# A written order for TensorE between the strided mix projection and the first feature tiles

## The chip, the cores and the metric

The kernel runs on one NeuronCore of a Trainium2 chip. The metric is the device time of one execution in microseconds (us), as the median over runs; lower is better. Below, TensorE (PE) multiplies matrices, VectorE (DVE) and ScalarE (ACT) work on elements and read TensorE's results from PSUM, GpSimd (POOL) works on elements in SBUF, and SyncE's queue (SP) issues the DMAs.

## The reference, cut to what matters

One encoder layer over 512 positions of width 1024, in float32: a mixer, then cross attention to 256 memory rows with 4 heads of width 256, then a gated feed-forward part, each followed by a LayerNorm over the sum with the scaled input. The stretch that is changed begins in the last part of the mixer's output projection and ends in the first features of the feed-forward part:

```
mixed = concat([rms_norm(out_a, g_win), rms_norm(out_b, g_dil)], -1)
h = layer_norm(ALPHA * h + mixed @ w_out, ln1_g, ln1_b)
mem_n = layer_norm(mem, mem_ln_g, mem_ln_b)
q = (h @ w_q).reshape(b, s, X_HEADS, X_HEAD_DIM)
k, v = the same of mem_n @ w_k and mem_n @ w_v
p = softmax(einsum('bshd,bmhd->bhsm', q, k) * X_HEAD_DIM ** -0.5)
o = einsum('bhsm,bmhd->bshd', p, v)
h = layer_norm(ALPHA * h + o.reshape(b, s, D_MODEL) @ w_o, ln2_g, ln2_b)
g = h @ w_gate            # then a convolution of width 3 along the positions
ff = (gelu(conv(g)) * (h @ w_up)) @ w_down
```

## The kernel before, in words

**Arithmetic.** A float32 product is computed as three products of a rounded part `hi` and a rest `lo`: hi x hi, hi x lo and lo x hi, all added in PSUM. So every operand exists as a pair. ScalarE makes `hi` by a copy (L139, L211, L1004), and VectorE or GpSimd makes `lo` by a subtraction (L141, L212, L1005). A weight tile of 128 x 1024 comes by one DMA of 512 KB into a `raw` buffer (three of them) and is split into `hi` and `lo` buffers (six of each). `w_cols` (L147) and `w_rows` (L152) do this; their argument `eng` names the engine for `lo`, VectorE if none is given.

**Tiles.** The 512 positions are four blocks of 128. A residual block `h[b]` holds 128 positions by 1024. `to_T` (L202) turns a block by eight transposes on TensorE (L206) into two PSUM banks; then come copies and subtractions (L211, L212) in two halves, into the pair `h1T` or `h2T` (`Uhi`, `Ulo`). `gemm_fm` (L162) multiplies 24 times with the positions as moving columns, `gemm_tm` (L173) 24 times with 512 weight columns moving. `layer_norm` (L131) takes statistics on VectorE, a reciprocal root on GpSimd (L112), and then two passes on VectorE in halves (L127, L129).

**PSUM.** There are eight banks: tag `g` two tiles of one bank, `t` and `o` one each, `s` two tiles of two banks. `f_tile` (L198) gives `t` and `g` by turns.

**The stretch.** The strided part of the mix projection (`mix_part`, L969 to L975) needs 12 matmuls for each half of each block; VectorE adds them to the residual, and norm and transposes of the block follow. The second half of the memory values (`proj_xv(1, ...)`, L978) stands behind this. The first three query tiles (L1055 to L1062) are computed in two halves of 256 positions, so that the first half needs only blocks 0 and 1; the others are whole. `attend_mem` (L1017) handles a head: for each block six matmuls of scores, a softmax (L1033 to L1039), two transposes (L1042), and for each pair of blocks the product with the values (L1049 to L1051) in 256 columns. The output projection (`proj_res_norm`, L983) runs over two column halves and four blocks; behind the second half come the norm and the transposes of each block. The first four feature products (two of `w_gate`, two of `w_up`) are computed in halves again (L1088 to L1096), and from feature 2 on (L1098) whole.

**What sets the order.** A planner places every instruction: it goes through the program with a timeline of its own and gives each engine, of what it holds to be ready, what stands first in the program. The engines then run their lists in that order. In a `manual_schedule` block the order of the named engine is that of the program text. Before the change such a block exists up to the end of the windowed part of the mix projection (L953); from the strided part on, the planner orders TensorE too, and moves matmuls of later stages ahead of waiting ones. DMAs are issued by SP in an order that the planner sets as well; a DMA whose buffer isn't free holds up those behind it.

Lines that the prediction names: L107 (the constants of a norm), L149 and L154 (weight loads), L160 (every matmul), L975 and L990 (PSUM onto the residual), L1109 to L1117 (a feature's evaluation), L1119 (constants of the last norm).

Of the kernel before, what the change touches and what calls it, by code (L numbers as in the profile page):

```python
# [13 lines left out]
ALU = mybir.AluOpType  # L14
# [59 lines left out]
def hymba_layer(ctx: ExitStack, tc: tile.TileContext, A, cst_d, out):  # L74
# [115 lines left out]
    gn = [0]  # L190

# [5 lines left out]

    def f_tile():  # L198
        gn[0] += 1
        return ps_tile("t", 1) if gn[0] % 3 == 1 else ps_tile("g", 2)  # L200
# [233 lines left out]
    def mmt(o, l, r, first, last, w=1.0):  # L434
        mm(o, l, r, first, last)
        tick(w)
# [324 lines left out]
    with tc.manual_schedule(engines={nc.tensor.engine}):  # L761
# [143 lines left out]
        def proj_xv(hf, pss):  # L905
            for i in range(KD // 2):
                w = w_rows(A["w_xv"][0], 2 * i, 2, hf * 512, 512)
                for b in range(2):
                    for k in (2 * i, 2 * i + 1):
                        whi, wlo = (t[:, k % 2, :] for t in w)  # L910
                        th, tl = (t[i][:, k % 2, b * P : (b + 1) * P] for t in memT)
                        mmt(pss[b], th, whi, k == 0, False)
                        mmt(pss[b], th, wlo, False, False)
                        mmt(pss[b], tl, whi, False, k == KD - 1)
            for b in range(2):
                nc.scalar.copy(vm[:, b, hf * 512 : (hf + 1) * 512], pss[b])
# [52 lines left out]
    wts = [load_dil(hf * 512) for hf in range(2)]  # L969
    for b in range(NB):  # L970
        for hf in range(2):
            ps = g_tile()
            mix_part(ps, wts[hf], b, 4, mm)
            hs = h[b][:, hf * 512 : (hf + 1) * 512]
            nc.vector.scalar_tensor_tensor(hs, ps, hp["d"][:, b : b + 1], hs, ALU.mult, ALU.add)  # L975
        layer_norm(h[b], g1, b1)
        to_T(h[b], h1T, b)
    proj_xv(1, [ps_tile("t", 1), ps_tile("o", 1)])  # L978

    def load_xo(c0, eng):  # L980
        return load_tm(A["w_xo"][0], c0, eng)

    def proj_res_norm(load, T, g, b_, dst):  # L983
        for hf in range(2):
            wts = load(hf * 512, nc.gpsimd)
            for b in range(NB):
                ps = f_tile()
                gemm_tm(ps, wts, T, blk(b))
                hs = h[b][:, hf * 512 : (hf + 1) * 512]
                nc.vector.scalar_tensor_tensor(hs, hs, ALPHA, ps, ALU.mult, ALU.add)  # L990
                if hf == 1:
                    layer_norm(h[b], g, b_)
                    to_T(h[b], dst, b)

    oT = T_pair()
    with pool("xat") as xp:
        w_xq = A["w_xq"][0]
        wq = {}

        def load_q(c):  # L1000
            wq[c] = w_cols(w_xq, c * P, nc.gpsimd)

        def split_ps(hi, lo, ps):
            nc.scalar.copy(hi, ps)  # L1004
            nc.vector.tensor_tensor(lo, ps, hi.bitcast(F32), ALU.subtract)  # L1005

        def evac_q(c, ps):
            wq["t", c] = [xpool.tile([P, S], F32R, tag="x", bufs=XB, name=n) for n in ("qh", "ql")]
            split_ps(*wq["t", c], ps)

        def proj_q(c):
            load_q(c)
            ps = f_tile()
            gemm_fm(ps, wq[c], h1T, 0, S)
            evac_q(c, ps)

        def attend_mem(hd):  # L1017
            qs = [wq["t", 2 * hd + cc] for cc in range(2)]
            kh, kl = split(kmT[:, 2 * hd : 2 * hd + 2, :], [P, 2, MEM], xpool, "x", XB, xpool, "x", XB)
            vh, vl = split(vm[:, :, hd * 256 : (hd + 1) * 256], [P, 2, 256], xpool, "x", XB, xpool, "x", XB)  # L1020
            for b2 in range(2):
                ph = xp.tile([P, 2, 256], F32R, tag="ph", bufs=2, name="ph")
                pl = xp.tile([P, 2, 256], F32R, tag="pl", bufs=2, name="pl")
                for b in (2 * b2, 2 * b2 + 1):
                    st_ = s_tile()
                    sp = st_[:, 0, :MEM]
                    t = slice(b * P, (b + 1) * P)
                    for cc in range(2):
                        mm(sp, qs[cc][0][:, t], kh[:, cc, :], cc == 0, False)
                        mm(sp, qs[cc][0][:, t], kl[:, cc, :], False, False)  # L1030
                        mm(sp, qs[cc][1][:, t], kh[:, cc, :], False, cc == 1)
                    mx = spool.tile([P, 1], F32, tag="mx", name="mx")
                    nc.vector.reduce_max(mx, sp, X, negate=True)  # L1033
                    nc.vector.tensor_scalar_mul(mx, mx, 1.0 / 16)
                    px = xp.tile([P, MEM], F32, tag="px", bufs=2, name="px")
                    dn = spool.tile([P, 1], F32, tag="dn", name="dn")
                    nc.scalar.activation(px, sp, AF.Exp, bias=mx, scale=1.0 / 16, accum_out=dn)
                    nc.vector.reciprocal(dn, dn)
                    nc.vector.tensor_scalar_mul(px, px, dn)  # L1039
                    tp = st_[:, 1, :MEM].rearrange("p (k t) -> p k t", k=2)  # L1040
                    for kb in range(2):
                        nc.tensor.transpose(tp[:, kb, :], px[:, kb * P : (kb + 1) * P], ident)  # L1042
                    t = slice((b % 2) * P, (b % 2 + 1) * P)
                    split_ps(ph[:, :, t], pl[:, :, t], tp)
                for cc in range(2):
                    ps = ps_tile("o", 1, [P, 256])
                    f = slice(cc * P, (cc + 1) * P)
                    for kb in range(2):
                        mm(ps, vh[:, kb, f], ph[:, kb, :], kb == 0, False)  # L1049
                        mm(ps, vh[:, kb, f], pl[:, kb, :], False, False)  # L1050
                        mm(ps, vl[:, kb, f], ph[:, kb, :], False, kb == 1)  # L1051
                    t = slice(b2 * 256, (b2 + 1) * 256)
                    split_ps(oT[0][:, 2 * hd + cc, t], oT[1][:, 2 * hd + cc, t], ps)

        first = [f_tile() for _ in range(3)]  # L1055
        for c in range(3):
            load_q(c)
        for s2 in range(2):
            for c in range(3):
                gemm_fm(first[c][:, s2 * 256 : (s2 + 1) * 256], wq[c], h1T, s2 * 256, 256)  # L1060
        for c in range(3):
            evac_q(c, first[c])  # L1062
        proj_q(3)
        attend_mem(0)
        proj_q(4)
        proj_q(5)
        attend_mem(1)
        proj_q(6)
        proj_q(7)
        attend_mem(2)  # L1070
        attend_mem(3)

    g2, b2 = gb_tiles(A["ln2_g"][0], A["ln2_b"][0])
    h2T = U_pair()
    proj_res_norm(load_xo, oT, g2, b2, h2T)
    mid.close()

    fp = ctx.enter_context(pool("ffn"))
# [118 lines left out]
```

## Time and profile before

| what | value |
|---|---|
| median of 3 runs | 975.44 us (975.24 to 977.02) |
| the profiled execution | 976.09 us, of which its span 974.0 |
| TensorE busy | 926.4 us, 95% |
| VectorE, ScalarE, GpSimd busy | 490.2, 366.4, 206.4 us |
| mean granted TensorE clock | 0.978 |
| HBM | 88.34 MB read, 4.19 MB written, 95 GB/s |

The page gives busy time for each engine, the chain of work that ended last, and groups of instructions by line. Rows of the order of time read: start, duration, engine, line, operation, output<-inputs, count, and in brackets the idle time before it with what ended it. The ends of matmuls are modelled: a row's duration runs past the start of the next one, so the distance of two starts is the cost of a matmul. `hi`, `lo` and `raw` are weight tiles, `Uhi` and `Ulo` the turned residual, `Thi` and `Tlo` the turned mix or attention output, `qh` and `ql` query tiles.

### The profile page before, as it was taken

What the parts mean: (1) busy time and instruction counts of PE and PEld (TensorE: products, weight loads), DVE (VectorE), ACT (ScalarE), POOL (GpSimd) and SP (SyncE); (2) the same over time, 40 slices, a digit from 0 to 9 for tenths busy, and PEclk for the clock granted to TensorE, in tenths of its full rate; (3) what the DMA queues carried; (4) which work ended last, traced back from release to release, by engine and by line L of the source; (5) the groups of instructions that cost most, each with busy time, mean ns of one, the idle gap of its engine ahead of it and who ended that gap; (6) DMA issues with size and microseconds to landing.
All of it is one profiled execution on the core that took longest, in us unless ns stands there. A gap on an engine that the chain in (4) does not pass through costs nothing.

```text
span 974.0 us, 12289 instructions
## 1 busy us (share of the span) xinstructions
PE 926.4 (95%) x4825; PEld 770.1 (79%) x4825; DVE 490.2 (50%) x866; ACT 366.4 (38%) x645; POOL 206.4 (21%) x135
## 2 busy tenths in 40 slices
PE   7989999999998899899899997999999999999996
PEld 5777887788776698688887786988888888788885
DVE  6683334524444564749435648454434443333346
ACT  3453444335544557322334512433323332232310
POOL 4253114511443232424541043000000000000001
PEclk7999999999999899999999997999999999999999
DMA  9542032313221227432531034233333333223201
GB/s 320 163 152 65 22 108 66 87 44 108 66 66 47 62 88 214 132 102 58 155 119 44 1 87 130 70 107 104 92 101 95 97 98 98 98 87 108 87 22 65
DMA packets 117066, 93.33 MB, mean 96 GB/s; under 512 B 12471, under 2 KB 100751, under 8 KB 117008
## 3 DMA queue, kind: packets, MB, share of 16 engines
q1 hardware_dynamic: 115106, 90.33, 30.6%
q10 hardware_dynamic: 1902, 2.21, 0.7%
q8 instruction: 38, 0.62, 0.3%
q14 instruction: 20, 0.16, 0.1%
HBM read 88.34 MB, written 4.19 MB: 95 GB/s over the span
## 4 chain that ended last, share of the span: by engine, by line
PE 59%; DVE 5%; ACT 2%; issue 2%; POOL 1%; DMA 0%; DVEq 0%; ACTq 0%; POOLq 0%
PE g L160 25%; PE s L160 15%; PE acc L160 12%; PE t L160 3%; PE o L160 2%; DVE h L129 1%; POOL lo L141 0%; ACT hi L139 0%; DVE lo L141 0%; PE s L206 0%; ACT pu L596 0%; PE t L505 0%; DMA raw<-in_w_xq_dram 0%; PE o L513 0%; DVE ka L704 0%
## 5 line engine op out<-in xcount | busy, mean ns | idle before, releaser
L139 ACT CAST hi<-raw 128x1024 fp32r<-128x1024 f32 x148 | 155.3, 1050 | 249.2 <-PE g L160 161.9
L141 DVE TENSOR_TENSOR lo<-raw,hi 128x1024 fp32r<-128x1024 f32 x114 | 141.7, 1244 | 147.8 <-ACT hi L139 145.7
L141 POOL TENSOR_TENSOR lo<-raw,hi 128x1024 fp32r<-128x1024 f32 x34 | 84.8, 2506 | 121.5 <-ACT hi L139 120.9
L112 POOL TENSOR_TENSOR rs<-ve,mhalf 128x1 f32<-128x1 f32 x18 | 15.6, 868 | 416.6 <-DVE ve L118 416.6
L160 PE MATMUL g<-Thi,hi 128*128 128x512 f32 x240 | 97.6, 407 | 2.1 <-DVE zs L367 2.1
L160 PE MATMUL g<-Thi,lo 128*128 128x512 f32 x240 | 97.0, 404 | 0.0
L160 PE MATMUL g<-Tlo,hi 128*128 128x512 f32 x240 | 96.7, 403 | 0.0
L160 PE MATMUL g<-Ulo,hi 128*128 128x512 f32 (+1 forms) x248 | 91.9, 371 | 1.1 <-DVE Ulo L212 1.0
L160 PE MATMUL g<-Uhi,hi 128*128 128x512 f32 (+1 forms) x248 | 91.7, 372 | 0.6 <-ACT Uhi L211 0.5
L160 PE MATMUL g<-Uhi,lo 128*128 128x512 f32 (+1 forms) x248 | 91.5, 369 | 0.0
L368 POOL TENSOR_TENSOR zs<-zs,rsn 128x512 f32<-128x512 f32 x29 | 57.5, 1983 | 148.4 <-DVE zs L367 148.4
L160 PE MATMUL g<-hi,Thi 128*128 128x512 f32 x200 | 82.7, 414 | 0.5 <-ACT Thi L299 0.3
L160 PE MATMUL g<-hi,Tlo 128*128 128x512 f32 x200 | 81.3, 408 | 1.8 <-DVE Tlo L327 1.8
L160 PE MATMUL g<-lo,Thi 128*128 128x512 f32 x200 | 78.5, 398 | 0.0
L160 PE MATMUL s<-Uhi,hi 128*128 128x512 f32 (+1 forms) x192 | 71.3, 371 | 0.0
L160 PE MATMUL s<-Ulo,hi 128*128 128x512 f32 (+1 forms) x192 | 71.3, 371 | 0.0
L160 PE MATMUL s<-Uhi,lo 128*128 128x512 f32 (+1 forms) x192 | 71.3, 371 | 0.0
L160 PE MATMUL acc<-hi 128*128 128x512 f32 x176 | 68.6, 390 | 0.8 <-DVE act L1117 0.8
L160 PE MATMUL acc<-hi,lo 128*128 128x512 f32 x176 | 68.5, 389 | 0.0
L160 PE MATMUL acc<-lo,hi 128*128 128x512 f32 x176 | 68.5, 389 | 0.0
L160 PEld LDWEIGHTS g<-Thi,hi 128*128 128x128 f32 x240 | 45.8, 191 | 13.5 <-DVE zs L367 2.9
L160 PEld LDWEIGHTS g<-Ulo,hi 128*128 128x128 f32 x248 | 48.8, 197 | 8.7 <-DVE Ulo L212 1.6
(259 smaller groups left out, 1737.4 us busy)
## 6 DMA issues: line engine op xcount, KB each, us to landing
raw<-in_w_in_dram SPq DMA_DIRECT2D x38, 512.0 KB, 3.9
raw<-in_w_gate_dram SPq DMA_DIRECT2D x22, 512.0 KB, 3.8
raw<-in_w_up_dram SPq DMA_DIRECT2D x22, 512.0 KB, 3.9
raw<-in_w_down_dram SPq DMA_DIRECT2D x22, 512.0 KB, 3.3
raw<-in_w_xk_dram SPq DMA_DIRECT2D x8, 512.0 KB, 3.9
raw<-in_w_xv_dram SPq DMA_DIRECT2D x8, 512.0 KB, 3.3
raw<-in_w_xq_dram SPq DMA_DIRECT2D x8, 512.0 KB, 4.1
raw<-in_w_xo_dram SPq DMA_DIRECT2D x8, 512.0 KB, 3.3
```

Source lines behind the costliest of these rows:

```text
L112: nc.gpsimd.tensor_tensor(out_, in_, mhalf, ALU.pow)
L129: nc.vector.scalar_tensor_tensor(th[i], th[i], rs, bt[i], ALU.mult, ALU.add)
L139: nc.scalar.copy(hi, raw)
L141: (eng or nc.vector).tensor_tensor(lo, raw, hi.bitcast(F32), ALU.subtract)
L160: nc.tensor.matmul(o, l, r, start=first, stop=last)
L368: nc.gpsimd.tensor_tensor(sh, sh, rsn, ALU.mult)
```

## The change

From the strided mix projection to the halves of the first features the program stands in `manual_schedule` blocks for TensorE, and its text is put into a new order:

- Mix: blocks 0, 1, 2, then the transposes of block 0, mix of block 3, transposes of block 1; first halves of three query tiles; transposes of block 2; three quarters of the second half of the memory values (now in one `s` tile); transposes of block 3; the last quarter; second halves of the query tiles.
- Cross attention by head, in four steps: `kv` splits keys and values, `x_scores` computes the scores of four blocks into one `s` tile and takes the softmax by pairs of blocks (one reduction for two), `x_turn` transposes all of a head's eight tiles into one `s` tile, `x_pv` multiplies with the values over all 512 positions into `o` and `t`. Query projections and other heads' steps stand between these.
- The softmax tiles `px` use the two buffers `gb`, which also hold the constants of the norms; the second norm's constants are loaded after them.
- Output projection: in the first column half, blocks 0 to 2 first take the six tiles of heads 0 to 2 and, behind head 3, the other two. In the second half the transposes of a block stand one to three stages behind its matmuls; those of blocks 2 and 3 stand between the feature products.
- The four feature products use `t`, `o`, `g`, `g` instead of `g`, `s`, `g`, `s`; the transpose of the convolution's weights stands behind the second of them.
- The weight tiles of the queries, the output projection and the first features are split by VectorE instead of GpSimd; those of the strided mix stay on GpSimd. `f_tile` is gone.

The core of the diff (the old stretch is printed above):

```
+        def proj_xv(hf, pss, i0=0, i1=KD // 2):
+            for i in range(i0, i1):
+                xv_rows(i, hf, pss, w_rows(A["w_xv"][0], 2 * i, 2, hf * 512, 512))
...
+    def proj_q(c):
+        ps = g_tile()
+        gemm_fm(ps, w_cols(w_xq, c * P), h1T, 0, S)
+        evac_q(c, ps)
...
+    def x_scores(hd):
+        kh, kl = KV[hd][0:2]
+        s = s_tile().rearrange("p a (c k) -> p (a c) k", c=2)
+        px = wpool.tile([P, NB, MEM], F32, tag="gb", bufs=2, name="px")
+        st_x[hd] = px
+        for b2 in range(2):
+            for b in (2 * b2, 2 * b2 + 1):
+                t = slice(b * P, (b + 1) * P)
+                for cc in range(2):
+                    qh, ql = QT[2 * hd + cc]
+                    mm(s[:, b, :], qh[:, t], kh[:, cc, :], cc == 0, False)
+                    mm(s[:, b, :], qh[:, t], kl[:, cc, :], False, False)
+                    mm(s[:, b, :], ql[:, t], kh[:, cc, :], False, cc == 1)
+            mx, dn = (spool.tile([P, 2], F32, tag=n, name=n) for n in ("mx", "dn"))
+            nc.vector.reduce_max(mx, s[:, 2 * b2 : 2 * b2 + 2, :], X, negate=True)
+            nc.vector.tensor_scalar_mul(mx, mx, 1.0 / 16)
...
+    def x_turn(hd):
+        px = st_x[hd]
+        tp = s_tile()
+        hl = st_x["t", hd] = [xp.tile([P, 2, S], F32R, tag=n, bufs=1, name=n) for n in ("ph", "pl")]
+        for kb in range(2):
+            for b in range(NB):
+                nc.tensor.transpose(tp[:, kb, b * P : (b + 1) * P], px[:, b, kb * P : (kb + 1) * P], ident)
+        for kb in range(2):
+            split_ps(hl[0][:, kb, :], hl[1][:, kb, :], tp[:, kb, :])
+
+    def x_pv(hd):
+        ph, pl = st_x["t", hd]
+        vh, vl = KV[hd][2:4]
+        pss = [ps_tile("o", 1), ps_tile("t", 1)]
+        for kb in range(2):
+            for cc in range(2):
+                f = slice(cc * P, (cc + 1) * P)
+                mm(pss[cc], vh[:, kb, f], ph[:, kb, :], kb == 0, False)
+                mm(pss[cc], vl[:, kb, f], ph[:, kb, :], False, False)
+                mm(pss[cc], vh[:, kb, f], pl[:, kb, :], False, kb == 1)
...
+    with tc.manual_schedule(engines={nc.tensor.engine}):
+        wts = [load_dil(hf * 512) for hf in range(2)]
...
+        dil(0)
+        dil(1)
+        dil(2)
+        to_T(h[0], h1T, 0)
+        dil(3)
+        to_T(h[1], h1T, 1)
+        first = [ps_tile("t", 1), g_tile(), g_tile()]
+        wq = [w_cols(w_xq, c * P) for c in range(3)]
+        for c in range(3):
+            gemm_fm(first[c][:, 0:256], wq[c], h1T, 0, 256)
+        to_T(h[2], h1T, 2)
+        xv = s_tile()
+        xv = [xv[:, i, :] for i in range(2)]
+        proj_xv(1, xv, 0, 3)
+        to_T(h[3], h1T, 3)
+        proj_xv(1, xv, 3, 4)
+        for c in range(3):
+            gemm_fm(first[c][:, 256:512], wq[c], h1T, 256, 256)
+            evac_q(c, first[c])
+        oT = T_pair()
+        kv(0)
+        x_scores(0)
+        proj_q(3)
+        x_turn(0)
+        kv(1)
+        x_scores(1)
+        x_pv(0)
+        proj_q(4)
+        x_turn(1)
+        proj_q(5)
+        x_pv(1)
+        kv(2)
+        x_scores(2)
+        proj_q(6)
+        x_turn(2)
+        proj_q(7)
+        x_pv(2)
+        kv(3)
+        x_scores(3)
+        w_xo = A["w_xo"][0]
+        wo = load_tm(w_xo, 0)
...
+        part = [g_tile(), g_tile()]
+        gemm_tm(part[0], wo, oT, blk(0), 0, 6)
+        x_turn(3)
+        gemm_tm(part[1], wo, oT, blk(1), 0, 6)
+        x_pv(3)
+        part.append(s_tile()[:, 0, :])
+        gemm_tm(part[2], wo, oT, blk(2), 0, 6)
+        for b in range(3):
+            gemm_tm(part[b], wo, oT, blk(b), 6, 8)
+            xo_evac(b, 0, part[b])
+        ps = ps_tile("t", 1)
+        gemm_tm(ps, wo, oT, blk(3))
+        xo_evac(3, 0, ps)
...
+        g2, b2 = gb_tiles(A["ln2_g"][0], A["ln2_b"][0])
+        h2T = U_pair()
+        wo = load_tm(w_xo, 512)
...
+        xo_1(0)
+        xo_1(1)
+        xo_1(2)
+        to_T(h[0], h2T, 0)
+        xo_1(3)
+        to_T(h[1], h2T, 1)
+        mid.close()
...
+    with tc.manual_schedule(engines={nc.tensor.engine}):
+        pre = [[None, ps_tile("t", 1)], [None, ps_tile("o", 1)], [None, g_tile()], [None, g_tile()]]
...
+        pre_gemm(0, 0)
+        pre_gemm(1, 0)
+        tp = s_tile()[:, 0, 0:88]
+        nc.tensor.transpose(tp, cw, ident[0:88, 0:88])
+        nc.vector.tensor_copy(cwT, tp)
+        to_T(h[2], h2T, 2)
+        pre_gemm(2, 0)
+        to_T(h[3], h2T, 3)
+        pre_gemm(3, 0)
+        for i in range(4):
+            pre_gemm(i, 1)
```

More of the change, by code (lines that the diff above doesn't have):

```diff
@@ L188, in ps_tile @@
         return gpool.tile(shape or [P, 512], F32, tag=tag, bufs=bufs, name=tag)
-    gn = [0]
     def g_tile():
@@ L196, in s_tile @@
         return ps_tile("s", 2, [P, 2, 512])
-    def f_tile():
-        gn[0] += 1
-        return ps_tile("t", 1) if gn[0] % 3 == 1 else ps_tile("g", 2)
     def to_T(t, T, b):
@@ L968, in hymba_layer @@
     h1T = U_pair()
-    wts = [load_dil(hf * 512) for hf in range(2)]
-    for b in range(NB):
-        for hf in range(2):
-            ps = g_tile()
[L973 to L1076, printed above, removed]
+    xs = ExitStack()
+    xp = xs.enter_context(pool("xat"))
+    w_xq = A["w_xq"][0]
+    QT = {}
+    KV = {}
+    st_x = {}
+    def split_ps(hi, lo, ps):
+        nc.scalar.copy(hi, ps)
+        nc.vector.tensor_tensor(lo, ps, hi.bitcast(F32), ALU.subtract)
+    def x2(shape, names):
+        return [xpool.tile(shape, F32R, tag="x", bufs=XB, name=n) for n in names]
@@ new lines, in evac_q, with kv @@
+    def evac_q(c, ps):
+        QT[c] = x2([P, S], ("qh", "ql"))
+        split_ps(*QT[c], ps)
+    def proj_q(c):
+        ps = g_tile()
+        gemm_fm(ps, w_cols(w_xq, c * P), h1T, 0, S)
+        evac_q(c, ps)
+    def kv(hd):
+        k_ = split(kmT[:, 2 * hd : 2 * hd + 2, :], [P, 2, MEM], xpool, "x", XB, xpool, "x", XB)
+        v_ = split(vm[:, :, hd * 256 : (hd + 1) * 256], [P, 2, 256], xpool, "x", XB, xpool, "x", XB)
+        KV[hd] = k_ + v_
+    def x_scores(hd):
[14 more added lines that the diff above has]
+            nc.vector.tensor_scalar_mul(mx, mx, 1.0 / 16)
+            for i in range(2):
+                b = 2 * b2 + i
+                nc.scalar.activation(
+                    px[:, b, :], s[:, b, :], AF.Exp, bias=mx[:, i : i + 1], scale=1.0 / 16,
+                    accum_out=dn[:, i : i + 1],
+                )
+            nc.vector.reciprocal(dn, dn)
+            for i in range(2):
+                b = 2 * b2 + i
+                nc.vector.tensor_scalar_mul(px[:, b, :], px[:, b, :], dn[:, i : i + 1])
@@ new lines, in x_turn @@
+    def x_turn(hd):
[17 more added lines that the diff above has]
+                mm(pss[cc], vh[:, kb, f], pl[:, kb, :], False, kb == 1)
+        for cc in range(2):
+            split_ps(oT[0][:, 2 * hd + cc, :], oT[1][:, 2 * hd + cc, :], pss[cc])
```

54 lines of the change are left out of this document (30 added, 24 removed).

## The prediction

> **What bounds the kernel now.** I read the page first, then the table of stretches, then TensorE's order of time around each stretch that loses something.
>
> ```profile
> span 974.0 us, 12289 instructions
> PE 926.4 (95%) x4825; PEld 770.1 (79%) x4825; DVE 490.2 (50%) x866; ACT 366.4 (38%) x645; POOL 206.4 (21%) x135
> ```
>
> TensorE (PE) is busy for 95% of the span, and the chain of waits runs mostly through it. So only time in which TensorE stands still or runs slowly can be won, and only where the change reaches. The change reaches from the first matmul of the strided mix projection (about 428 us) to the last of the first feature tiles (about 627.7 us). Columns of the next view: stretch, its length, then busy time of PE, PEld, DVE, ACT, POOL (with counts), granted PE clock, DMA share, GB/s.
>
> ```profile
> 468.60:476.40 7.80, 5.10 (x30) 4.75 (x29) 5.08 (x4) 1.17 (x2) 3.14 (x2) 0.78 0.67 182
> 476.40:509.50 33.10, 33.10 (x192) 29.23 (x192) 8.21 (x16) 12.44 (x19) 14.31 (x6) 1.00 0.35 117
> 509.50:560.40 50.90, 47.87 (x289) 40.14 (x287) 31.09 (x95) 24.43 (x68) 4.79 (x2) 1.00 0.08 25
> ...
> 591.50:606.10 14.60, 8.89 (x40) 8.20 (x40) 14.60 (x24) 2.22 (x3) 5.46 (x4) 0.65 0.62 184
> ...
> 428.00:627.70 199.70, 188.09 (x1081) 164.07 (x1080) 119.41 (x222) 71.23 (x131) 57.59 (x28) 0.97 0.28 83
> ```
>
> Busy time hides short pauses, so I price the work itself, from rows where TensorE runs without a break: the chain's piece of 24 matmuls of 512 columns, the first and last of 33 matmuls of 256 columns, and a group of eight transposes with what follows it.
>
> ```profile
> 633.34 5.44 PE s L160 x24
> ```
> ```profile
> 623.75 0.28 PE L160 MATMUL g<-Uhi,hi 128*128 128x256 f32 x1
> ...
> 627.59 0.28 PE L160 MATMUL s<-Uhi,lo 128*128 128x256 f32 x1
> ```
> ```profile
> 583.49 1.03 PE L206 MATMUL s<-cst,h 128*128 128x128 f32 x8
> 584.28 0.47 PE L160 MATMUL g<-hi,Thi 128*128 128x512 f32 x1
> ```
>
> That is 5.44/24 = 0.227 us for 512 columns, 3.84/32 = 0.120 us for 256, and 0.79/8 = 0.099 us for a transpose. The loops of the code between the two ends issue 456 matmuls of 512 columns (96 strided mix, 48 memory values, 120 queries, 192 output), 528 of 256 (144 queries, 96 scores, 96 times values, 192 features) and 97 transposes: 103.4 + 63.4 + 9.6 = 176.4 us. The stretch took 199.7. So 23.3 us are lost, and that is the most that any order can win here. Where they are lost:
>
> ```profile
> 469.63 0.63 PE L206 MATMUL s<-cst,h 128*128 128x128 f32 x4 [0.86 <-issue]
> 472.35 0.66 PE L206 MATMUL s<-cst,h 128*128 128x128 f32 x4 [1.85 <-DVE h L129]
> 473.12 0.42 PE L160 MATMUL g<-Uhi,lo 128*128 128x256 f32 x1
> 473.34 0.42 PE L160 MATMUL g<-Uhi,hi 128*128 128x256 f32 x1
> ```
> ```profile
> 595.77 1.85 PE L206 MATMUL s<-cst,h 128*128 128x128 f32 x8 [4.18 <-DVE h L129]
> 598.29 0.80 PE L160 MATMUL g<-Uhi,hi 128*128 128x256 f32 x2 [0.53 <-ACT Uhi L211]
> 600.09 0.58 PE L160 MATMUL g<-Ulo,hi 128*128 128x256 f32 x1 [1.00 <-DVE Ulo L212]
> ```
>
> Both LayerNorm ends have one shape: the transposes wait for VectorE's last step of the norm (L129), and then the clock is low (0.78 and 0.65), so that 256 columns take 0.22 us instead of 0.12. In 468.6 to 476.4, 22 matmuls of 256 and 8 transposes are worth 3.4 us: 4.4 lost. In 591.5 to 606.1, 31 matmuls and 9 transposes are worth 4.6: 10.0 lost. The other 8.9 are shared by cross attention (3.0 shown as idle in 509.5 to 560.4) and short pauses that busy time hides; 476.4 to 509.5, q projections alone, has no idle time.
>
> **The change part by part.** *TensorE's work.* Only the product with the values changes: 96 matmuls of 256 columns (11.5 us) become 48 of 512 (10.9). That is -0.6.
>
> *Weight splits leave GpSimd.* The `lo` halves of 20 weight tiles (8 of w_xq, 8 of w_xo, 4 of the first features) move to VectorE. What one costs on each engine, and what GpSimd's did to the norm:
>
> ```profile
> L141 DVE TENSOR_TENSOR lo<-raw,hi 128x1024 fp32r<-128x1024 f32 x9 | 11.0, 1220 | 14.6 <-ACT hi L139 14.6
> ```
> ```profile
> L141 POOL TENSOR_TENSOR lo<-raw,hi 128x1024 fp32r<-128x1024 f32 x20 | 50.0, 2513 | 87.8 <-ACT hi L139 87.2 <-POOL rs L112 0.5
> ```
> ```profile
> 466.59 5.16 POOL L141 TENSOR_TENSOR lo<-raw,hi 128x1024 fp32r<-128x1024 f32 x2
> ```
> ```profile
> 444.50 0.75 DVE L975 SCALAR_TENSOR_TENSOR h<-g,rad__3380,h 128x512 f32<-128x512 f32 x1 [0.64 <-PE g L160]
> 445.29 0.69 DVE L134 BATCH_NORM_STATS2 st<-h 128x6 f32<-128x512 f32 x1
> ...
> 446.33 1.41 DVE L127 SCALAR_TENSOR_TENSOR h<-h,mv,gb 128x512 f32<-128x512 f32 x2
> ...
> 448.91 0.74 DVE L129 SCALAR_TENSOR_TENSOR h<-h,rs,gb 128x512 f32<-128x512 f32 x1
> ...
> 467.17 5.12 DVE L129 SCALAR_TENSOR_TENSOR h<-h,rs,gb 128x512 f32<-128x512 f32 x2
> ```
>
> VectorE gets 20 x 1.22 = 24.4 us more. In return the pair of L129, which under GpSimd's two splits took 5.12 us, has no split beside it; undisturbed, such a pair is worth 1.41 like L127. A norm from the PSUM result to the finished block is then 444.50 to 449.65 less the 0.6 of another block's step in between: 4.5 us.
>
> *First norm.* New order: three blocks of mix, transposes of block 0, the fourth block, transposes of block 1, half of three q projections (72 x 0.12 = 8.6 us), transposes of block 2, three quarters of the memory values (36 x 0.227 = 8.2), transposes of block 3. Block 3 now has 0.8 + 8.6 + 0.8 + 8.2 = 18.4 us, and a wait for block 1, against a norm of 4.5: the old wait and its low clock go (-4.4). What is late next: the q projection right behind the transposes of block 1 needs their halves. From the two engines' rows of such a hand-over:
>
> ```profile
> 584.56 0.59 ACT L211 CAST Uhi<-s 128x512 fp32r<-128x512 f32 x1 [9.07 <-PE s L206]
> 585.90 0.59 ACT L211 CAST Uhi<-s 128x512 fp32r<-128x512 f32 x1 [0.76 <-DVE Ulo L212]
> ```
> ```profile
> 585.18 0.69 DVE L212 TENSOR_TENSOR Ulo<-s,Uhi 128x512 fp32r<-128x512 f32 x1 [4.08 <-ACT Uhi L211]
> ```
>
> TensorE is free at 584.28 and the first half is there at 585.87: 1.6 us. The second half comes 1.35 later, under 12 matmuls (1.44). Nothing covers the 1.6; behind that matmul on TensorE stands everything else. VectorE also has more per mix block (2 x (0.75 + 0.69) + 0.4 + 2 x 1.41 = 6.1 us) than TensorE (5.44), the values no longer lie between the blocks, and there are only two `g` banks. The lag is 0.7 a block, plus 1.4 for block 0's halves and 2.4 for two q weights: about 5 at the fourth block, against 2.7 us (the other bank) + 0.8 of cover. So 0 to 2.5; I take 1.0, nearer none, because the planner may put the bank's step ahead. New loss 1.6 + 1.0 = 2.6. Net -1.8.
>
> *Cross attention.* Softmax of a pair of blocks, first step to last, in today's trace (VectorE):
>
> ```profile
> 499.14 0.43 DVE L1033 TENSOR_REDUCE mx<-s 128x1 f32<-128x256 f32 x1 [3.15 <-PE s L160]
> ...
> 501.19 0.35 DVE L1039 TENSOR_SCALAR px<-px,dn 128x256 f32<-128x256 f32 x1
> ...
> 492.89 0.69 DVE L1005 TENSOR_TENSOR ql<-t,qh 128x512 fp32r<-128x512 f32 x1 [4.67 <-ACT qh L1004]
> ```
>
> That is 2.4 us; with one reduction for both blocks ahead of the first exponential, at most 0.43 more: 2.8. Its transposes now come a projection (5.44) later, or at the last head 18 matmuls (4.08): covered. The values product comes after 2.9 us at head 0, and later elsewhere, against two hand-overs of 1.35. Tightest is head 1's scores, which need q tile 3 just 0.8 us after its projection; today the `ql` of that tile is ready at 493.58, 2.1 us after its last matmul: 0 to 1.3, I take 0.5, and as much again for the other heads. Some 17 changes of stage at 0.08 (0.31 instead of 0.227 us for the first matmul behind transposes) are 1.4. Of the 8.9 lost outside the norms I keep 1.9 as now, plus 1.4 and 1.0 to 1.2: 4.5. Saved 4.4; bounds 1.8 (the shown 3.0 idle goes, and q tile 3 costs its 1.3) and 6.5 (only 2.4 stays).
>
> *Loads.* The norm's constants share their two buffers with the softmax tiles now, so their DMAs wait on SP's queue for the transposes of heads 2 and 3, and four w_xo loads stand behind them. Cover: 90 matmuls of 512 from those transposes to the second half of w_xo, 20.4 us.
>
> ```profile
> raw<-in_w_xo_dram SPq DMA_DIRECT2D x8, 512.0 KB, 3.3
> ```
>
> Five such transfers in a row are 16.5, with a split 18.9: nothing, by 1.5 us. Past that cover it costs what it is late.
>
> *Second norm.* Behind the third output block stand transposes 0, block 3's matmuls, transposes 1, two feature halves (5.8), transposes 2, one half (2.9), transposes 3: 18.2 us with the 1.6 wait for block 1. VectorE's work in that time is two norms (2 x 4.5), three blocks' halves (3 x 1.4), at most four splits (4.9): 18.1. It fits, barely. So -10.0, and new: 1.6, plus one step of the norm (0.7) in VectorE's queue ahead of it, 2.4 with its hand-over; bounds 1.6 and 3.8. Net -7.6.
>
> *Feature banks.* Feature 2 needs the bank of feature 1's gate, behind which only 24 x 0.12 = 2.9 us of matmuls lie. Today those three steps take 621.59 to 624.38, 2.8 us:
>
> ```profile
> 621.59 0.77 ACT L1109 ACTIVATE c<-g,cwT 128x512 f32<-128x512 f32 x1
> ...
> 623.63 0.75 DVE L1113 SCALAR_TENSOR_TENSOR c<-g,cwT,c 128x511 f32<-128x511 f32 x1
> ```
>
> I take +0.2; bounds 0 and 1.2 (a split in front).
>
> **The sum.** -0.6 - 1.8 - 4.4 - 7.6 + 0.2 = -14.2. The profiled execution took 976.1 for a span of 974.0, so 2.1 lie around it; 974.0 - 14.2 + 2.1 = 961.9. It was 0.65 above the median of 975.44: 961.2.
>
> **Rivals.**
> (a) *The new waits lower the clock.* The trace shows it low after pauses of 0.86 and 1.85 within 4 us, and shows the attention stretch, with 3.0 us of pauses scattered over 51, at 1.00. The new waits of 1.6 to 2.6, in one piece, lie between. A low clock met 22 matmuls at the first norm and 31 at the second, at 0.1 us each 2.2 and 3.1: 961.2 + 5.3 = 966. [...]
> (b) *The waits move instead of going.* If VectorE, whose 18.1 of 18.2 us has no reserve, comes 5 us late to block 3's second norm, that and one low clock give back 7.6, and the time is 969. For it: the margin. Against: TensorE also slips by its own waits, which gives VectorE time.
> (c) *Slower.* The 24.4 us of splits stand in VectorE's in-order queue ahead of hand-overs that TensorE's fixed order can no longer step around. All on the path: 961.2 + 24.4 = 986. It decides from 14.2/1.22 = 12 of the 20 splits. For it: every hand-over passes VectorE. Against: VectorE is busy 119.4 of 199.7 us, and splits are asked for early.
>
> **Chances.** The forecast 0.62 (own range, from the bounds: 957 to 968), (a) 0.15, (b) 0.15, (c) 0.08. A measurement here tells about 0.2% from no change, 973.5 to 977.4. Faster 0.88, same 0.04 (the edges of b and c), slower 0.08. The range goes from 955.5 to 971, so that it holds (a) and (b) and leaves out (c) and the outer edges.
>
> **What would show it.** Right: no wait on L129 ahead of transposes; two waits of 1.6 to 2.6 us for Uhi or Ulo, behind block 1's transposes of each norm; granted clock near 1.00 throughout; the stretch from the first strided mix matmul to the last half-width feature matmul about 185.5 us; GpSimd with nothing but the root and four splits. Wrong: a pause over 3 us anywhere in it, a low clock (a), a transposes wait on L129 for block 3 (b), or waits on L141 splits adding to over 10 us (c).

## The result, and the profile after

| | before | changed |
|---|---|---|
| median | 975.34 us (974.97 to 977.02, 4 runs) | 992.47 us (991.72 to 993.04, 4 runs) |
| span of the profiled execution | 974.0 us | 989.9 us |
| mean granted TensorE clock | 0.978 | 0.972 |

The ratio is 1.016 (95% interval 1.0141 to 1.0178): the change made the kernel slower by 17 us. The prediction said 961.2, with a range of 955.5 to 971.

The page after, its head and the line of engines:

```profile
span 989.9 us, 12130 instructions
...
PE 928.5 (94%) x4777; PEld 772.0 (78%) x4777; DVE 495.4 (50%) x846; ACT 363.5 (37%) x629; POOL 156.7 (16%) x115
```

GpSimd lost its 50 us of splits, as it should. TensorE has 48 instructions less and is busy for 2.1 us more. The table of stretches shows where, with the columns of the prediction's first table. The rows are the first norm with values and query halves; attention with the first half of the output projection; its second half with the second norm and the feature halves; and the three together.

```profile
428.20:490.05 61.85, 56.59 (x321) 50.23 (x319) 43.48 (x63) 17.89 (x23) 3.87 (x4) 0.94 0.31 94
490.05:590.60 100.55, 83.87 (x394) 70.09 (x394) 45.82 (x86) 34.87 (x72) 0.00 (x0) 0.92 0.15 48
590.60:645.60 55.00, 52.19 (x330) 47.42 (x330) 37.10 (x57) 16.53 (x22) 3.65 (x4) 0.97 0.39 115
...
428.20:645.60 217.40, 192.65 (x1043) 167.74 (x1042) 126.40 (x204) 69.29 (x117) 7.53 (x8) 0.94 0.26 78
```

With the prediction's prices (0.227, 0.120 and 0.099 us for 512 columns, 256 columns and a transpose) the work in these rows is worth 53.1, 74.5 and 49.9 us; the last row also holds eight matmuls of feature 2, 1.8 us, which the planner moved in. So 8.8 us are lost at the first norm (4.4 before), 26.0 in attention (8.9 before in all that lies outside the norms) and 5.1 at the second norm (10.0 before). That is 16.6 more, less the 0.6 that the product with the values saves: 16.0, against 15.9 between the two spans.

TensorE's waits in the changed stretch (428 to 646 us), grouped (total us, times, longest):

```profile
PE s L160 <- ACT px L1012: 9.8, 4, 3.4
PE t L160 <- DVE Ulo L206: 6.6, 2, 4.6
PE s L160 <- ACT hi L139: 3.6, 2, 2.0
PE s L160 <- DVE lo L141: 3.3, 4, 1.2
PE t L160 <- ACT Uhi L205: 1.4, 2, 0.8
```

No transposes wait for the last step of a norm (L129 in both kernels). That part worked. In its place stand 24.7 us of waits. The same view of the kernel before, from 428 to 628 us, adds up to 11.3 with four groups of 0.2 to 0.7 that are left out:

```profile
PE s L206 <- DVE h L129: 6.0, 2, 4.2
PE o L160 <- DVE Tlo L1005: 1.5, 3, 0.8
PE g L160 <- DVE Ulo L212: 1.0, 1, 1.0
PE s L206 <- issue: 0.9, 1, 0.9
...
```

So 13.4 of the loss is waiting. The rest, some 3 us, isn't shown as idle time; the granted clock over the stretch is 0.94, where it was 0.97. Single waits in TensorE's order of time:

```profile
457.51 0.58 PE L160 MATMUL t<-Ulo,hi 128*128 128x256 f32 x1 [4.58 <-DVE Ulo L206]
492.18 0.38 PE L160 MATMUL s<-hi,qh 128*128 128x256 f32 x1 [2.02 <-ACT hi L139]
493.63 0.39 PE L160 MATMUL s<-lo,qh 128*128 128x256 f32 x1 [1.07 <-DVE lo L141]
499.35 0.58 PE L160 MATMUL s<-hi,qh 128*128 128x256 f32 x1 [3.38 <-ACT px L1012]
...
541.32 0.39 PE L160 MATMUL s<-hi,qh 128*128 128x256 f32 x1 [2.14 <-ACT px L1012]
...
563.49 0.39 PE L160 MATMUL s<-hi,qh 128*128 128x256 f32 x1 [2.14 <-ACT px L1012]
...
617.34 0.58 PE L160 MATMUL t<-Ulo,hi 128*128 128x256 f32 x1 [2.06 <-DVE Ulo L206]
```

Three places come out of this.

*The second pair of blocks of each head* (499.35, 541.32, 563.49 and one more at 516.43) waits for the exponentials of the first pair, whose results it doesn't read. It only writes its scores into the same `s` tile that the first pair's softmax reads, in the tile's other bank. Head 0 waits 3.38 us instead of 2.1 because a table load of ScalarE (L1012, 1.28 us at 496.98) stands ahead of its first exponential.

*The first scores of heads 0 and 1* wait for the `hi` of keys (L139). ScalarE's order of time shows why it is late:

```profile
490.08 1.04 ACT L139 CAST hi<-raw 128x1024 fp32r<-128x1024 f32 x1 [1.35 <-PE g L160]
491.03 0.58 ACT L974 CAST qh<-g 128x512 fp32r<-128x512 f32 x1
491.50 0.62 ACT L139 CAST hi<-kmT 128x512 fp32r<-128x512 f32 x1
```

The planner placed the cast of a weight tile for a later projection ahead of the query and key casts. That cast needs a buffer which the projection just running gives back with its last matmul, so ScalarE stood still for 1.35 us with the key cast behind it.

*The query halves at the first norm* wait 4.58 us for block 1's `Ulo`. VectorE has no gap there:

```profile
451.93 1.22 DVE L141 TENSOR_TENSOR lo<-raw,hi 128x1024 fp32r<-128x1024 f32 x1
453.06 0.69 DVE L134 BATCH_NORM_STATS2 st<-h 128x6 f32<-128x512 f32 x1
453.67 1.21 DVE L141 TENSOR_TENSOR lo<-raw,hi 128x1024 fp32r<-128x1024 f32 x1
454.79 0.75 DVE L1052 SCALAR_TENSOR_TENSOR h<-g,rad__3380,h 128x512 f32<-128x512 f32 x1
455.45 1.41 DVE L129 SCALAR_TENSOR_TENSOR h<-h,rs,gb 128x512 f32<-128x512 f32 x2
456.78 0.68 DVE L206 TENSOR_TENSOR Ulo<-s,Uhi 128x512 fp32r<-128x512 f32 x1
```

From 451.93 to 456.78 two weight splits and the steps of other blocks stand in its in-order queue, ahead of the one subtraction that TensorE waits for; the copy `Uhi` that it needs was done at 452.49.

### The profile page after: what moved, and what is told of

It is laid out like the page before. It is cut to its first block, busy times and chain, and to the rows that moved or that the text cites. A ratio compares the mean times of both kernels' runs of the same rounds, so it can differ in the third digit from the quotient of the medians.

```text
span 989.9 us, 12130 instructions
## 1 busy us (share of the span) xinstructions
PE 928.5 (94%) x4777; PEld 772.0 (78%) x4777; DVE 495.4 (50%) x846; ACT 363.5 (37%) x629; POOL 156.7 (16%) x115
## 3 DMA queue, kind: packets, MB, share of 16 engines
q1 hardware_dynamic: 115106, 90.33, 30.1%
## 4 chain that ended last, share of the span: by engine, by line
PE 59%; DVE 5%; ACT 3%; issue 2%; POOL 1%; DVEq 0%; ACTq 0%; POOLq 0%
PE g L160 26%; PE s L160 15%; PE acc L160 12%; PE t L160 2%; DVE lo L141 2%; PE o L160 1%; ACT hi L139 1%; PE s L200 1%; ACT px L1012 0%; ACT pu L590 0%; PE t L499 0%; PE o L507 0%; DVE ka L698 0%; POOL x L363 0%; POOL zs L362 0%
## 5 line engine op out<-in xcount | busy, mean ns | idle before, releaser
L141 DVE TENSOR_TENSOR lo<-raw,hi 128x1024 fp32r<-128x1024 f32 x134 | 166.2, 1242 | 174.6 <-ACT hi L139 167.4
L139 ACT CAST hi<-raw 128x1024 fp32r<-128x1024 f32 x148 | 155.3, 1050 | 231.5 <-PE g L160 164.5
L160 PE MATMUL g<-Uhi,hi 128*128 128x512 f32 (+1 forms) x264 | 97.4, 369 | 0.0
L160 PE MATMUL g<-Ulo,hi 128*128 128x512 f32 (+1 forms) x264 | 96.8, 367 | 0.0
L160 PE MATMUL g<-Uhi,lo 128*128 128x512 f32 (+1 forms) x264 | 96.6, 366 | 0.0
L160 PE MATMUL g<-lo,Thi 128*128 128x512 f32 x208 | 81.6, 398 | 0.0
L160 PE MATMUL s<-Uhi,lo 128*128 128x512 f32 x160 | 62.3, 389 | 0.0
L160 PE MATMUL s<-Ulo,hi 128*128 128x512 f32 x160 | 62.3, 389 | 0.0
L160 PE MATMUL s<-Uhi,hi 128*128 128x512 f32 x160 | 62.2, 389 | 0.0
L160 PEld LDWEIGHTS g<-Uhi,hi 128*128 128x128 f32 x264 | 50.7, 192 | 7.8
L160 PEld LDWEIGHTS g<-Uhi,lo 128*128 128x128 f32 x264 | 50.4, 191 | 8.1
```

Source lines behind the costliest of these rows:

```text
L139: nc.scalar.copy(hi, raw)
L141: (eng or nc.vector).tensor_tensor(lo, raw, hi.bitcast(F32), ALU.subtract)
L160: nc.tensor.matmul(o, l, r, start=first, stop=last)
```

## The experiments

All runs but the last five keep the written order; "wait" means a TensorE wait in the stretch. Ratios are to the kernel before, with 95% intervals. Its median beside these runs was 975.3 to 977.0 us, so differences between times of separate sessions are uncertain by up to 2 us.

### The scores of a head ahead of its softmax

```
                     mm(s[:, b, :], ql[:, t], kh[:, cc, :], False, cc == 1)
+        for b2 in range(2):
             mx, dn = ...
```

> The changed kernel with one edit: a head's 24 score matmuls are all issued ahead of both softmax pairs. Theory A, the wait of the second pair belongs to the shared PSUM tile (its first matmul waits until everything that reads the tile so far, the first pair's reduction and exponentials, is done): the four waits on the exponentials (3.38 + 2.10 + 2.14 + 2.14 = 9.8 us) go, and with them some of the low clock at 490 to 510 us; 992.5 falls to 979 to 983. Rival B, the second pair is held by something else that comes out at the same time (the key splits, the queue of VectorE), or the softmax, which now starts 1.4 us later, comes too late for the transposes: 990 to 993.

Measured: 981.72 us, ratio 1.0044 (1.0027 to 1.0062), 10.7 less than the changed kernel. Its ten runs lie at 978.8 to 980.1 us and at 983.3 to 984.2 us, so the median is uncertain by some 2 us. All four waits for the exponentials are gone. The transposes now wait for the softmax instead, 0.29 and 0.86 us; the waits at the norms (4.59 and 2.08) and for head 0's keys (2.02 and 1.07) are as they were. So writing all scores before any of them is read removes the wait. Whether it was the tile or the bank that made it, this run doesn't say.

### The second pair in a tile of its own

```
-        s = s_tile().rearrange("p a (c k) -> p (a c) k", c=2)
+        sa = s_tile()[:, 0, :].rearrange("p (c k) -> p c k", c=2)
+        sb = g_tile().rearrange("p (c k) -> p c k", c=2)
...
+            s = (sa, sb)[b2]
```

> The changed kernel, its order of text and of TensorE unchanged, but the second pair of a head's scores goes into a g tile of its own instead of the second bank of the s tile. Theory A, the wait on the exponentials belongs to the tile and not to the data, the bank or the order: the four waits (9.8 us) go as they did when the matmuls were put ahead of the softmax, 978 to 984. Rival B, writing scores next to a running softmax is slow in itself: 989 to 993.

Measured: 978.55 us, ratio 1.0023 (1.0007 to 1.0038), 13.9 less than the changed kernel. The order of scores and softmax is the changed kernel's; only the tile is another. TensorE's grouped waits:

```profile
PE t L160 <- DVE Ulo L206: 6.6, 2, 4.6
PE s L160 <- ACT hi L139: 3.6, 2, 2.0
PE s L160 <- DVE lo L141: 3.3, 4, 1.2
PE t L160 <- ACT Uhi L205: 1.4, 2, 0.8
```

The four other groups of the changed kernel stand unchanged to the tenth, and the fifth, 9.8 us, is missing. The two pairs lie in different banks in both kernels, so the wait belongs to the tile: in this program a write to one bank of it waits for the readers of the other. The time saved, 13.9, is 4.1 more than the waits. From 490 to 510 us its rows are slow (256 columns in 0.21 us) from 495.5 to 498.9 and from 509.3 on; in the changed kernel the granted clock is 0.53 from 494 to 496 us and 0.50 from 499 to 503.

### Keys and values split a stage earlier

```
         proj_xv(1, xv, 3, 4)
+        kv(0)
...
-        kv(0)
         x_scores(0)
+        kv(1)
         proj_q(3)
```

and likewise for `kv(2)` and `kv(3)`.

> The changed kernel with the key and value splits of a head written one stage earlier in the program (those of the next head right behind a head's scores, those of head 0 ahead of the query tiles' second halves). Theory: the first score matmuls wait for these splits (2.02 + 1.07 + 1.56 + 1.18 + 0.55 + 0.54 = 6.9 us) only because they stand behind a weight cast and a weight split; early, they are ready: 5 to 7 us less, 985 to 988. Rival: at heads 1 to 3 the query tile ql stands behind the same weight split and is needed at the same place, so that only head 0's 3.1 us go: 989 to 990.

Measured: 988.49 us, ratio 1.0112 (1.0095 to 1.0129), 4.0 less than the changed kernel. The 6.9 us of waits for the key splits are gone, but the waits for the exponentials grow:

```profile
PE s L160 <- ACT px L1012: 12.7, 4, 5.1
```

So 2.9 of the 6.9 came back at the next wait, and two new waits for a query tile took 1.1.

### Both together

The edits of the first and the third run.

> The changed kernel with both edits that helped singly: score matmuls ahead of the softmax, and key and value splits one stage earlier; TensorE's order still fixed. If the two costs are separate, 992.5 - 10.7 - 4.0 gives 977 to 978, about the kernel before, and the gap to the 962 of the planner's order (some 15 us) lies in the first norm's wait on Ulo (5.3), the second's (2.8), the query tiles behind weight splits and the low clock after each. Rival, the costs stand for each other (a score matmul that no longer waits for keys waits for the query tile or for the softmax's transposes): 980 to 983.

Measured: 973.16 us, ratio 0.9958 (0.9945 to 0.9971), 19.3 less than the changed kernel, where the two alone give 10.7 + 4.0 = 14.7. The 4.6 beyond the sum would fit what the earlier splits alone had given back at the exponentials and the query tile; with the first run uncertain by 2 us, this isn't shown. Attention's waits are down to 2.8 us, from 16.7; what is left stands at the norms:

```profile
460.58 0.58 PE L160 MATMUL t<-Ulo,hi 128*128 128x256 f32 x1 [4.59 <-DVE Ulo L206]
...
598.11 0.58 PE L160 MATMUL t<-Ulo,hi 128*128 128x256 f32 x1 [2.06 <-DVE Ulo L206]
```

### The weight splits back on GpSimd

```
-        gemm_fm(ps, w_cols(w_xq, c * P), h1T, 0, S)
+        gemm_fm(ps, w_cols(w_xq, c * P, nc.gpsimd), h1T, 0, S)
```

and the same for the three first query tiles, the output projection and the four feature weights.

> The changed kernel with the lo halves of its 20 weight tiles (w_xq, w_xo, first features) back on GpSimd. Theory: splits of 1.22 us in VectorE's queue make the 4.58 us wait on Ulo at the first norm (three splits stand ahead there, 3.7 us) and lengthen the waits on the key splits (3.3 us in all): 5 to 7 us less, 985 to 988. Rival: GpSimd's splits stretch the norms again as in the kernel before (5.12 us instead of 1.41 for a pair of steps) and cost as much as they give: 990 to 995.

Measured: 1002.7 us, ratio 1.0257 (1.0239 to 1.0276), 10.2 more than the changed kernel. So the splits cost less on VectorE than on GpSimd; what they cost at all, this run doesn't say. The waits for `Ulo` grow from 6.6 to 9.5 and those for key `lo` from 3.3 to 5.0. One norm step shows a way in which this happens, GpSimd's row and then VectorE's:

```profile
449.00 2.40 POOL L141 TENSOR_TENSOR lo<-raw,hi 128x1024 fp32r<-128x1024 f32 x1 [5.60 <-ACT hi L139]
```
```profile
449.92 2.70 DVE L127 SCALAR_TENSOR_TENSOR h<-h,mv,gb 128x512 f32<-128x512 f32 x2
```

Beside a GpSimd split the pair takes 2.70 instead of 1.41 us; 1.48 of it lie before the split's end at 451.40. Why the pair is slower there, the rows don't show.

### Block 1's transposes inside block 3's matmuls

On top of both edits, block 1 is transposed between the two halves of block 3's matmuls, at both norms, and no longer behind them:

```
-        dil(3)
-        to_T(h[1], h1T, 1)
+        dil(3, lambda: to_T(h[1], h1T, 1))
...
-        xo_1(3)
-        to_T(h[1], h2T, 1)
+        xo_1(3, lambda: to_T(h[1], h2T, 1))
```

> TensorE's order still fixed, with the two attention edits (973.2 so far), and in each norm the transposes of block 1 put into the middle of block 3's matmuls instead of behind them, so that 12 matmuls of 512 columns (2.7 us) cover the hand-over to Uhi and Ulo, as the planner does it. Theory: what is left over the planner's 962 are the two waits behind those transposes (0.7 + 4.6 and 0.8 + 2.1 us) and the low clock after each: 962 to 966. Rival, the wait at the first norm is three weight splits in VectorE's queue and stays behind them wherever the transposes stand: 968 to 973.

Measured: 972.91 us, ratio 0.9957 (0.9941 to 0.9973), 0.25 from the run without it: no difference. The half of a block's matmuls, 2.7 us, now lies between transposes and their use, and yet 1.78 + 2.88 us of waits stand at the first norm, in place of 0.68 + 4.59. VectorE's queue there:

```profile
455.15 1.22 DVE L141 TENSOR_TENSOR lo<-raw,hi 128x1024 fp32r<-128x1024 f32 x1
456.29 0.68 DVE L206 TENSOR_TENSOR Ulo<-s,Uhi 128x512 fp32r<-128x512 f32 x1
...
458.15 1.22 DVE L141 TENSOR_TENSOR lo<-raw,hi 128x1024 fp32r<-128x1024 f32 x1
...
460.60 1.21 DVE L141 TENSOR_TENSOR lo<-raw,hi 128x1024 fp32r<-128x1024 f32 x1
461.74 0.68 DVE L206 TENSOR_TENSOR Ulo<-s,Uhi 128x512 fp32r<-128x512 f32 x1
```

Two splits and four steps of other blocks' norms stand between the two subtractions of block 1: bringing the transposes forward brought only the first of them forward.

### First halves interleaved

On top of that, the first halves of two query tiles, and of two features, run by turns: the row tiles 0 to 3 of both, then 4 to 7. What needs the first tile's late subtraction then stands twelve matmuls further back.

```
-        for c in range(3):
-            gemm_fm(first[c][:, 0:256], wq[c], h1T, 0, 256)
+        for k in (0, 4):
+            for c in range(2):
+                gemm_fm(first[c][:, 0:256], wq[c], h1T, 0, 256, k, k + 4)
+        gemm_fm(first[2][:, 0:256], wq[2], h1T, 0, 256)
```

> The fixed order with the scores of a head ahead of its softmax, the key and value splits a stage earlier, block 1's transposes inside block 3's matmuls at both norms, and now also the first halves of query chunks 0 and 1, and of the first two feature chunks, interleaved: k 0 to 3 of both, then k 4 to 7, so that the matmuls that need the late blocks' transposes come 8 matmuls (about 1.8 us by 0.227 us each) later. Cover theory: what TensorE lacks at a norm is work that needs only early blocks; the 1.78 + 2.88 us of waits ahead of Uhi and Ulo at the first norm and the 3.2 us at the second shrink to under 2 us together, the clock stays above 0.95, and the time falls from 972.9 to 964 to 968. Queue theory: VectorE's queue is full from the first block's statistics on, the last block's low half comes when it comes, the waits stay within 1 us of what they were and the time stays at 970 to 973.

Measured: 968.94 us, ratio 0.9913 (0.9892 to 0.9934), 4.0 less. It lies between the two theories' figures, nearer the first. (The 0.227 us of the expectation is the price of 512 columns; these matmuls have 256, 0.120 us at the full clock.) The waits that are left at the first norm:

```profile
455.61 0.39 PE L160 MATMUL t<-Ulo,hi 128*128 128x256 f32 x1 [1.77 <-DVE Ulo L206]
461.06 0.39 PE L160 MATMUL t<-Ulo,hi 128*128 128x256 f32 x1 [0.83 <-DVE Ulo L206]
```

The second wait fell by 2.05, the first did not move; at the second norm 1.33 and 0.73 are left of 1.33, 0.90 and 0.99. Work in between helps where there is any: the first wait at each norm still has the same matmuls ahead of it.

### The same text without a written order

```
-    with tc.manual_schedule(engines={nc.tensor.engine}):
+    if True:
```

at both blocks from the strided projection on: the planner orders TensorE too, as before the change.

> The changed kernel without the two blocks that fix TensorE's order behind the windowed mix projection: same text, same tiles, same engines, but the planner orders TensorE too. Theory F, the fixed order is what costs: matmuls of other stages fill the waits again, 976 to 982. Theory A, the waits lie in the text itself (shared tile, splits) and the planner does not see them as long as they are: little less than 992, 986 to 993.

Measured: 961.97 us, ratio 0.9851 (0.9827 to 0.9875), 30.5 less than the changed kernel. The longest waits in the stretch:

```profile
PE s L1152 <- DVE h L1099: 1.3, 1, 1.3
PE g L160 <- ACT Thi L974: 1.0, 2, 0.5
PE g L160 <- DVE ql L975: 0.9, 1, 0.9
```

All of them add up to 5.5 us; the stretch, with a clock of 1.00, takes

```profile
429.80:614.67 184.87, 179.54 (x1036) 156.96 (x1035) 123.71 (x202) 67.69 (x114) 7.52 (x8) 1.00 0.30 92
```

with only one matmul of feature 2 (0.2 us) in it. VectorE is as full at the first norm as in the changed kernel (10.00 of the 10 us from 450 to 460; there 9.97), but TensorE's order of time shows matmuls moved in where one would wait. Head 0's scores, the end of the first pair and the start of the second:

```profile
490.41 0.28 PE L160 MATMUL s<-hi,qh 128*128 128x256 f32 x1
...
492.88 0.28 PE L160 MATMUL s<-hi,ql 128*128 128x256 f32 x1
493.00 0.40 PE L160 MATMUL g<-Ulo,hi 128*128 128x512 f32 x1
...
499.60 0.39 PE L160 MATMUL g<-Uhi,hi 128*128 128x512 f32 x1
499.82 0.28 PE L160 MATMUL s<-hi,qh 128*128 128x256 f32 x1
```

Between the two pairs stand 30 matmuls of query projections, 6.8 us, in which the first pair's softmax ends. The first scores come late enough too: from 485.08 on TensorE works on a projection, and neither the first matmul at 490.41 nor any other waits for the key's halves. The two waits of the changed kernel have no place to arise.

The edit frees TensorE alone, but the planner's lists for the other engines change with it. Block 1's first `Ulo` starts at 452.62 us on VectorE, 3.0 us after its transposes began; in the changed kernel it starts at 456.78, 6.0 us after. So the 30.5 us are the cost of the fixed order together with the lists that the planner makes around it.

### The planner's order with the earlier edits

Scores ahead of the softmax and keys split earlier, then in another run block 1's transposes inside block 3's matmuls alone, each without a written order.

> The new text with the planner's order for TensorE and the two edits (score matmuls ahead of the softmax, key and value splits earlier). In the planner's order the waits are filled with other matmuls and only 4.9 us of idle time are left in the stretch, none of it on keys or exponentials: the edits give nothing, 960 to 963. Rival, planner and fixed order have the same costs and only their cover differs, so that the edits free matmuls for other gaps: 955 to 959.

Measured: 962.39 us, ratio 0.9849 (0.9825 to 0.9873): no difference from 961.97. What was worth 19.3 us in a written order is worth nothing where the order steps around it.

> The new text with the planner's order and only the move of block 1's transposes into the middle of block 3's matmuls, at both norms. The planner has moved those of the first norm there by itself; at the second norm 0.75 + 1.25 + 0.17 us of waits are left (on Uhi, on the convolution weights' buffer, on Ulo). Theory, the text decides only where the planner does not see the wait: 960 to 962. Rival, the forced place displaces better cover: 963 to 966.

Measured: 960.28 us, ratio 0.9837 (0.981 to 0.9864), the lowest median here. Its 1.7 less than the run without that edit is inside the intervals of the two, so a gain from the edit isn't shown; that it beats both kernels is.

### Text and engine apart

The old text with only the 20 splits moved to VectorE, and the new text in the planner's order with the 20 splits on GpSimd.

```
-            wts = load(hf * 512, nc.gpsimd)
+            wts = load(hf * 512, None)
...
-            wq[c] = w_cols(w_xq, c * P, nc.gpsimd)
+            wq[c] = w_cols(w_xq, c * P)
```

is the core of the first edit; the second joins those of "The same text without a written order" and "The weight splits back on GpSimd".

> The kernel before, in its own text and with the planner's order, with only the engine part of the change: the lo halves of the same 20 weight tiles on VectorE instead of GpSimd. Theory G, GpSimd's splits stretch the steps of both norms that the transposes wait for (5.12 us for a pair worth 1.41, and alike at the second norm), so that the engine part is a good deal of what the planner's order of the new text gains over 976: 964 to 970. Rival H, the new text is it (late transposes with matmuls of other stages between, one step for a head): 973 to 977.

Measured: 969.89 us, ratio 0.9929 (0.9907 to 0.9951).

> The new text of the kernel with the planner's own order on TensorE (962.0 measured with the 20 weight splits on VectorE), and those 20 splits back on GpSimd: it separates the text from the engine. On the old text the splits on VectorE were worth 975.4 to 969.9. [...] If the planner's order steps around the longer hand-over, it loses under 2 us: 962 to 964, and the text alone carries the whole gain.

Measured: 968.17 us, ratio 0.9911 (0.9886 to 0.9937), 6.2 more than with the splits on VectorE (961.97), not under 2. With these, the change falls apart into three. Against the kernel before, by the ratios:

| | splits on GpSimd | splits on VectorE |
|---|---|---|
| old text, planner's order | 0 | -0.7% |
| new text, planner's order | -0.9% | -1.5% |
| new text, written order | +2.6% | +1.6% |

One per cent is 9.8 us. Moving the splits is worth 0.6 to 0.7% in the planner's order and 1.0% in the written one; the new text, in the planner's order, 0.8 to 0.9%. Both gain, and nearly add. The written order costs 3.1 to 3.5%, 30 to 34 us.

## Why the prediction was wrong

**The written order was priced mainly at the norms.** The sum expected a span of 974.0 - 14.2 = 959.8; it was 989.9, so 30.1 too little. By the prediction's own parts: attention was to keep 4.5 us of loss and kept 26.0 (+21.5); the first norm was to lose 2.6 and lost 8.8 (+6.2); the second 2.4, and it lost 5.1 (+2.7). That is 30.4, less the feature banks' 0.2.

**Cross attention: the failed step, "a projection (5.44) later", "covered".** It followed the softmax to its transposes and found cover. It did not ask what stands between the two pairs of scores: 12 matmuls of the second pair, behind a softmax that reads the same tile. That is 9.8 us of waits and, by the run with a tile of its own, 13.9 us of time. A row which the prediction quoted held the sign of it: the second `Uhi` copy of the kernel before stood still for 0.76 us "<-DVE Ulo", behind a subtraction whose result it doesn't read. The copy shares with it only the tiles: `s`, which both read, and `Uhi`, of which it writes the half that the subtraction doesn't read. The row was used for a duration alone. Block 1's second copy in the changed kernel has the same wait:

```profile
457.49 0.59 ACT L205 CAST Uhi<-s 128x512 fp32r<-128x512 f32 x1 [3.82 <-DVE Ulo L206]
```

**Head 1's q tile: wrong place, wrong size.** "0 to 1.3, I take 0.5" was the price for `ql`. No `ql` wait is in the changed kernel. Heads 0 and 1 waited for the keys' halves instead, 2.02 + 1.07 and 1.56 + 1.18, and heads 2 and 3 0.55 and 0.54: 6.9 us. The step counted the matmuls between a projection and its use; the queue of the engine that makes the halves, with a weight cast at its head that waits for a buffer, was not walked through. In the two runs with this cured, `ql` did wait, for 0.87 and 0.59 us: the term was there, hidden behind a larger one. The run with both edits of attention takes 19.3 us less than the changed kernel, most of the 21.5.

**First norm: "1.6", "0 to 2.5; I take 1.0".** The old wait for L129 went as said. Its successor was to cost 2.6 and cost 0.68 + 4.58 in waits and, with the slow clock (0.50 from 457 to 462 us), 8.8. The lag of VectorE was worked out as 5 us and a cover of 3.5 taken off, as if TensorE met it at a bank. It waited for no bank. It met the lag at the subtraction right behind block 1's transposes, 4.3 us late behind two splits and other blocks' steps, and nothing covers that. The bound of 2.5 was the mis-sized term. The planner did not put the right step ahead, as the text hoped. That this queue is the cause is read from the rows; no run took the splits out of it without putting them on GpSimd.

**Second norm: right in kind.** 0.75 + 2.06 = 2.8 us of waits, 2.4 predicted, inside the bounds of 1.6 to 3.8. With the slow clock behind them (0.50 from 617 to 619 us) the loss is 5.1; the old one was 10.0. The gain is 4.9, not 7.6.

**Splits, loads, feature banks.** Moving the splits to VectorE is a gain of 0.6 to 1.0% in all three pairs of runs, of which the prediction had priced only the shorter norm. No TensorE wait in the stretch points at a late load or a feature bank.

**The rivals.** (a), a low clock behind the new waits, happened (0.74 from 490 to 510 us, 0.50 from 617 to 619); 13.4 of the 16.6 us more are waits, and the clock's share of the rest was not taken apart. (b) did not: no transposes waited for a norm. (c) had the sign and not the mechanism: with the splits back on GpSimd the kernel is slower still. What (c) said in passing, hand-overs "that TensorE's fixed order can no longer step around", is what the runs show; it was tied to the splits, given a price of 24.4 at most and a chance of 0.08, while 9.8 of the 24.7 us of waits have no split ahead of them.

**What the 961.2 was right about.** The new text in the planner's order takes 961.97, and its stretch 184.9 us where 185.5 were named. The prediction had worked out what the text allows and taken the order for free. That the single terms were right doesn't follow from the sum; so close an agreement may be luck.

**Still open.** The best written order here (968.94) lies 7.0 us behind the planner's. Its waits in the stretch add up to 7.5 us against 5.5. Of the other 5.0 the clock may be most: it is 0.83 from 450 to 460 us and again from 500 to 510, against 1.00 in the planner's order, and 17% of these 20 us are 3.4, an estimate. No run here tells how much of the changed kernel's loss is the clock alone.

## What to carry to other kernels

In a written order nothing steps around a late hand-over: for each matmul of it, walk the in-order queue of the engine that makes its operand, and not only the distance in matmuls. Look for writes into a tile that another engine is still reading another part of; giving the parts tiles of their own, or writing all before any is read, was worth 11 to 14 us here in the written order. Where a planner can order the engine, change the text and the engines first and measure that alone: here those two parts gained 1.5%, and the fixed order gave back 3.1%.

## What the runs showed of the hardware

The same pauses did not always bring the same clock. Windows of the changed kernel around the second pair of head 2 and of head 3, with nearly the same two pauses (0.55 and 0.54 us, then 2.14) ahead of each:

```profile
541.30:544.00 2.70, 2.68 (x13) 2.61 (x14) 0.94 (x4) 0.00 (x0) 0.00 (x0) 0.61 0.02 6
544.00:546.00 2.00, 2.00 (x7) 1.56 (x6) 0.80 (x3) 1.02 (x4) 0.00 (x0) 0.67 0.00 0
```
```profile
563.00:566.00 3.00, 2.51 (x17) 2.34 (x18) 1.53 (x5) 0.43 (x2) 0.00 (x0) 1.00 0.04 14
```

Behind the one the clock is 0.61 and 0.67, and from 541.9 to 545.3 us 256 columns take 0.21 and 512 columns 0.43 us; behind the other it stays at 1.00. It is alike between runs. In the run with both edits of attention, waits of 1.39 us at head 0's transposes and 0.59 us in head 1's first scores leave the clock at 1.00 (500 to 510 us); in the run with first halves interleaved, 1.39 and 0.58 us at the same places are followed by 0.63 and 0.51 (500 to 504 us). So the length of a pause does not decide alone.
